# A priority flag on one weight split, and later planner due times for four inverses, in a two-layer decoder trunk

## The chip, the cores and the metric

One core of a Trainium2 chip runs the whole trunk. The metric is the device time of one execution in microseconds (us), as the median of several. TensorE (PE in the rows) multiplies matrices, VectorE (DVE), ScalarE (ACT) and GpSimd (POOL) work element by element, and SyncE (SP) issues the DMAs.

## What is computed

An even layer (RWKV-7 with 16 heads, S5, memory attention) is followed by an odd layer (Mamba-2, latent attention, memory attention). Both have one input projection, one output projection and a residual add; a norm ends the trunk. Model width and sequence length are 1024, all in fp32. The part of the reference that this case turns on is RWKV's step:

```
def step(state, inp):
    r_t, w_t, k_t, v_t, kk_t, b_t = inp
    sa = -jnp.einsum('bhij,bhj->bhi', state, kk_t)
    state = (state * w_t[:, :, None, :] + sa[..., None] * b_t[:, :, None, :]
             + v_t[..., None] * k_t[:, :, None, :])
    return state, jnp.einsum('bhij,bhj->bhi', state, r_t)
```

The kernel does it in blocks of 128 steps. Within a block the dependence on `sa` is a triangular system, and the inverses of its 32x32 diagonal parts are needed before the block's state can be computed.

## The kernel before

**Dense products.** Projections run as fp32 in three products of rounded halves: x is kept as `xhi` and `xlo`, and each 128x512 weight tile `w` is loaded by a DMA (`load_w`, L322), cast to `wh` on ACT (L405) and reduced to the remainder `wl` on DVE (L406; both in `split`). Each step of 128 rows is three matmuls of 128x512 (`mm<-xhi,wh`, `mm<-xlo,wh`, `mm<-xhi,wl`, L180), called *products* below. `w` has two buffers, `wh` and `wl` four each. Eight steps, 24 products, fill one bank "mm" (there are two), which ACT and DVE then evacuate into a tile `ev` (two buffers) that a DMA stores.

**What sets the order.** `Flow` (from L160) plans PE's order by hand: generators ("streams") with ranks yield the event they wait for, `F.done(event, dt)` sets when an event is due, and the clock `now` advances by a cost for each matmul. The stream of the best rank that is due goes next; the dense products, `self.bg` with rank 9 (`dense`, L340), fill what is left. `keep_in_program_order` makes that PE's order on the chip. The other engines and SP's DMA issues are put in order by the framework's scheduler, which goes by dependencies, its own estimates and priorities. On the chip every engine works its list strictly in order and waits wherever an operand is missing.

**The first weight tiles.** `rw_items` (L876) begins the dense list. Its first item takes the tiles 24 and 8, already loaded as `self.w0`, and the tile `win[0]`, the *third*, whose split goes through `load_w`; its products write a bank "g" for the first half of the sequence.

**RWKV's units.** `rw_streams` (L920) works 16 units (head pair p, half h), n = 0 to 15. For each, `stream_a` forms `ga` (`rw_prep0`) and calls `rw_inv0` (L690): SP sends `ga` out to `d_in` (L699, four DMAs) and back in another layout as `ai` (L702), POOL solves by 62 operations on `ti` (L711, L713), SP stores `ti` to `d_out` (L715) and fetches the inverse as `xt` (L718, four DMAs). Then `stream_i` runs `rw_inv1` (L720): DVE transposes `xn<-xt` (L728), and PE's first products with it are `g<-xn,ga`. `stream_b` forms the other operands (transposes of `rv`, `tg`, `km`; copies `tok` on ACT, L684), and `stream_s` runs the recurrence. `stream_a` may start unit n when unit n-3's recurrence is done, because there are three tiles `xt`. The event ("V", n), at which the planner takes unit n's inverse as ready, is due HW = 14 planner microseconds after `pool_t`, which advances by at least HV = 16 for each unit.

**After RWKV.** S5 reads parameters (`s5_params`, products `bbr`, `bbi`, L1307), and `mem_load` (L1033) fetches `mh` and `ml`, 1 MB each, into a pool on the space that S5's temporary tiles leave, so those DMAs wait for the last use of these, DVE's `bbi` of L1307. 24 *memory products* `mm<-mh,wh` (and `ml,wh`, `mh,wl`, 128x256) stand in the dense list, due S5M = 13 planner microseconds after the load was asked for. S5's own first work on PE is transposes `g<-ident,rn` (L184).

Of the kernel before, what the change touches and what calls it, by code (L numbers as in the profile page):

```python
# [19 lines left out]
P = 128  # L20
# [112 lines left out]
HW = 14  # L133
# [26 lines left out]
class Flow:  # L160
# [4 lines left out]
    def __init__(self, tc, banks):  # L165
        self.tc, self.nc = tc, tc.nc
        self.now = 0.0
        self.at, self.streams, self.n = {}, [], 0
        self.banks = banks
        self.free = {t: [0.0] * n for t, n in banks.items()}  # L170
# [76 lines left out]
class Item:  # L247
# [1 line left out]


    def __init__(self, src=None, kt=8, x=None, evac=None, ev=None, m=P, halves=(0, 1), wait=None, hwait={},
                 pre=None, post=None, gen=None, first=True, last=True, kwait={}):
        self.src, self.kt, self.x, self.evac, self.ev, self.m = src, kt, x, evac, ev, m
        self.halves, self.wait, self.hwait, self.pre, self.post, self.gen = halves, wait, hwait, pre, post, gen
        self.first, self.last, self.kwait = first, last, kwait


class Tiles(list):
# [7 lines left out]
class K:  # L266
# [52 lines left out]
        return pool.tile(list(shape), F32, name=tag, bufs=self.flow.banks[tag])  # L319


    def load_w(self, parts, src, kt, m=P, pool=None):  # L322

        nc = self.nc
        src = src.rearrange("p (k m) -> p k m", k=kt)
        ks = 4 * P // m
        for k in range(0, kt, ks):
            n = min(ks, kt - k)
            v = lambda t: t[:, 0:n * m].rearrange("p (k m) -> p k m", k=n)
            w = v(self.wp.tile([P, 4 * P], F32, name="w", bufs=2))  # L330
            nc.sync.dma_start(w, src[:, k:k + n])
            hi, lo = (v((pool or self.wp).tile([P, 4 * P], F32R, name=x, bufs=4 if pool else WB)) for x in ("wh", "wl"))
            self.split(hi, lo, w)
            for p, t in zip(parts, (hi, lo)):
                p.extend(t[:, i] for i in range(n))
            yield k + n

    def dense(self, items):

        F = self.flow  # L340
        acc, w, ends = {}, {}, {}
        live = [0]

        def pieces():
            for n, i in enumerate(items):
                w[n], ends[n] = (Tiles(), Tiles()), []
                if i.src is not None:
                    for e in self.load_w(w[n], i.src, i.kt, i.m):
                        ends[n].append(e)
                        live[0] += 1  # L350
                        yield n if e == i.kt else n - 0.5
                else:
                    yield n
        todo = pieces()
        at = [-1]

        def fill(n):

            while at[0] < min(n, len(items) - 1) or live[0] < WB and at[0] < min(n + 2, len(items) - 1):
                at[0] = next(todo)  # L360

        for n, cur in enumerate(items):
            fill(n)
            if cur.wait is not None:
                yield cur.wait
            if cur.pre:
                cur.pre()
            if cur.gen:
                yield from cur.gen(w[n])
                live[0] -= len(ends[n])  # L370
            else:
                for h in cur.halves:
                    if h in cur.hwait:
                        yield cur.hwait[h]
                    if cur.first:
                        yield ("mm", 1)
                        acc[h] = self.bank("mm")
                    (hi, lo), m, kt = w[n], cur.m, cur.kt
                    for k in range(kt):
                        if k in cur.kwait:  # L380
                            yield cur.kwait[k]
                        if k == 0 or k in cur.kwait:
                            xh, xl = cur.x(h)
                            ps = acc[h][:, 0:xh.shape[-1]]
                        for j, (l, r) in enumerate(((hi, xh), (hi, xl), (lo, xh))):
                            F.matmul(ps[0:m], lhsT=l[:, k], rhs=r[:, k], start=(cur.first and k == 0 and j == 0),
                                     stop=(cur.last and k == kt - 1 and j == 2))
                        if h == cur.halves[-1] and k + 1 in ends[n]:
                            live[0] -= 1
                            fill(n)  # L390
                        if k < kt - 1:
                            yield 0
                    if cur.last:
                        cur.evac(h, ps)
                        F.rel("mm", 2.0)
            if cur.ev:
                F.done(cur.ev, 7.0)
            if cur.post:
                cur.post()
            del w[n]  # L400
            yield 0
# [478 lines left out]
    def rw_items(self, np_, x, rd, zd, npairs=8):  # L880

        nc, F = self.nc, self.flow
        win = self.I["w_ev_in"]
        item = lambda ct, ev: Item(win[ct], 8, x, self.shift_evac(ct, rd[ct]), ev)
        gate = lambda p: Item(win[35 + p], 8, x, self.keep_evac("gate", zd[p]), ("gate", p))

        def first(w):
            evs = [(self.shift_evac(ct, rd[ct], np_.tile([P, 1], F32, name="bd%d" % ct)), ev)
                   for ct, ev in ((24, "lat"), (8, ("k", 0)), (0, None))]
            for h, tags in enumerate((("mm", "mm", "g"), ("g", "mm", "mm"))):  # L890
                yield ("raw", h)
                xh, xl = x(h)
                self.raw[h] = []
                for tag, (hi, lo), e in zip(tags, (*self.w0, w), evs):
                    yield (tag, 1)
                    ps = self.bank(tag)
                    for k in range(8):
                        for j, (l, r) in enumerate(((hi, xh), (hi, xl), (lo, xh))):
                            F.matmul(ps, lhsT=l[:, k], rhs=r[:, k], start=(k == 0 and j == 0), stop=(k == 7 and j == 2))
                        yield 0  # L900
                    self.raw[h].append((ps, tag, *e))
                F.done(("raw1", h))
        items = [Item(win[0], 8, gen=first)]
        for p in range(npairs):
            if p:
                items += [item(8 + p, ("k", p)), item(p, None)]
            items.append(item(16 + p, ("v", p)))
            if p:
                items.append(gate(p - 1))
        items[1].hwait = {0: ("x0", 0), 1: ("x0", 1)}  # L910
        items.append(gate(npairs - 1))
        return items

    def rw_streams(self, cp, wk, rd, zd, npairs=8):


        nc, F = self.nc, self.flow
# [5 lines left out]
        pool_t = [0.0]  # L923
# [9 lines left out]
        def raw(n, nm, c, bufs):  # L933
            p, h = units[n]
            t = self.pp.tile([P, HT], F32, name=nm, bufs=bufs)
            nc.sync.dma_start(t, rd[c + p][:, h * HT:(h + 1) * HT])
            return t

        def latents():

            lat = self.pp.tile([P, T], F32, name="ai", bufs=1)
            nc.sync.dma_start(lat, rd[24])
            nc.scalar.activation(lat[0:64], lat[0:64], AF.Tanh)
            for h in (1, 0):
                s = slice(h * HT, (h + 1) * HT)
                lt = self.pp.tile([P, 2, HT], F32R, name="lt", bufs=1)
                for i, (hs, ls) in enumerate(((slice(0, 64), slice(64, 128)), (slice(64, 128), slice(0, 64)))):
                    nc.scalar.copy(lt[hs, i], lat[hs, s])
                    nc.vector.tensor_tensor(lt[ls, i], lat[hs, s], lt[hs, i].bitcast(F32), A.subtract)
                nc.sync.dma_start(ltd[h], lt.bitcast(F32))  # L950
            return lt

        def stream_a():
            yield "lat"
            lt = latents()
            for n, (p, h) in enumerate(units):
                yield [("k", p), E("S", n - 3), E("B", n - 1)]
                if n % 2 == 0 and n:
                    lt = self.pp.tile([P, 2, HT], F32R, name="lt", bufs=1)
                    nc.sync.dma_start(lt.bitcast(F32), ltd[h])  # L960
                k = raw(n, "rk", 8, 2)
                yield from self.rw_prep0(st[n], p, lt, lora(p), k, wk)
                F.done(("A", n), 2.5)
                self.rw_inv0(st[n], n, wk)
                pool_t[0] = max(pool_t[0], F.now + 10) + HV
                F.done(("V", n), pool_t[0] + HW - F.now)

        def stream_i():
            for n in range(nh):
# [1522 lines left out]
```

## Time and profile before

| | before |
|---|---|
| median of three runs | 2689.26 us (2682.48 to 2698.61) |
| the profiled execution | 2699.3 us, span 2697.5 us |
| granted PE clock, mean | 0.953 of full |
| PE busy | 2520.6 us, 93% |
| DVE, ACT, POOL busy | 66%, 46%, 21% |

PE is busy in 93% of the span, so a change tells in two ways: through the time in which PE stands, and through the time in which it runs at the lower of its two levels (a granted clock of 0.50 is 1.2 GHz, 1.00 is 2.4 GHz). A row of the timeline gives start, duration, engine, line, operation, what it writes and reads, how many were joined (x4), and in brackets how long the engine had stood before it and what released it.

### The profile page before, as it was taken

How to read it: one execution, taken by the hardware profiler on the slowest of the kernel's cores; microseconds unless marked ns; L12 is line 12 of the kernel's file. 1: busy time of each engine (PE TensorE's matmuls, PEld its weight loads, DVE VectorE, ACT ScalarE, POOL GpSimd, SP SyncE). 2: the span in 40 equal slices, each digit the busy share in tenths (PEclk: the TensorE clock that was granted, in tenths of full speed). 3: DMA queues.
4: the chain of work that ended last, by engine and by line, in shares of the span. 5: the costliest groups of instructions: out<-in, count | busy, mean ns of one | idle time of the engine just before them, and what ended most of it. 6: DMA issues, size and time to landing. Idle time of an engine off the chain costs nothing. (4 is left out here: it accounts for less than half of the span.)

```text
span 2697.5 us, 42287 instructions
## 1 busy us (share of the span) xinstructions
PE 2520.6 (93%) x15058; PEld 2036.5 (75%) x15058; DVE 1771.6 (66%) x3639; ACT 1249.7 (46%) x2445; POOL 563.2 (21%) x1287
## 2 busy tenths in 40 slices
PE   7979999999999988988999998999999989999997
PEld 5757777787777867775678776777777768887786
DVE  9846667676666646777556456798644987777432
ACT  7533344343444333455444345545434645666443
POOL 3432353334434410000000111122111120000011
PEclk9988899998999999988999999999999989999999
DMA  4432323333333244464574564252445332114543
GB/s 150 130 93 86 87 83 91 106 103 87 92 97 88 74 128 145 124 205 149 172 255 141 164 187 138 69 128 87 125 146 197 117 109 65 58 51 144 164 135 100
DMA packets 263859, 328.27 MB, mean 122 GB/s; under 512 B 88016, under 2 KB 135248, under 8 KB 263136
## 3 DMA queue, kind: packets, MB, share of 16 engines
q1 hardware_dynamic: 260736, 319.39, 38.5%
q0 software_dynamic: 1280, 4.20, 0.4%
q8 instruction: 119, 1.95, 0.3%
q10 hardware_dynamic: 1632, 1.98, 0.3%
q14 instruction: 92, 0.75, 0.1%
HBM read 232.59 MB, written 92.90 MB: 121 GB/s over the span
## 5 line engine op out<-in xcount | busy, mean ns | idle before, releaser
L406 DVE TENSOR_TENSOR wl<-w,wh 128x512 fp32r<-128x512 f32 (+2 forms) x410 | 273.9, 672 | 295.7 <-ACT wh L405 291.4
L405 ACT CAST wh<-w 128x512 fp32r<-128x512 f32 (+2 forms) x410 | 241.8, 594 | 417.8 <-PE mm L180 259.8
L180 PE MATMUL mm<-xhi,wh 128*128 128x512 f32 x832 | 364.1, 438 | 10.5 <-ACT xhi L474 6.5
L180 PE MATMUL mm<-xlo,wh 128*128 128x512 f32 x832 | 339.7, 408 | 3.8 <-DVE xlo L497 2.4
L180 PE MATMUL mm<-xhi,wl 128*128 128x512 f32 x832 | 338.8, 407 | 0.0
L180 PE MATMUL mm<-x1h,wh 128*128 128x512 f32 (+1 forms) x608 | 249.7, 411 | 23.3 <-ACT craw L1829 16.6
L711 POOL TENSOR_TENSOR titmp<-ai,ti 128x60 f32<-128x60 f32 (+24 forms) x496 | 167.4, 338 | 412.1 <-DMA ai<-d_in 374.5
L180 PE MATMUL mm<-x1h,wl 128*128 128x512 f32 (+1 forms) x608 | 240.9, 396 | 0.0
L180 PE MATMUL mm<-x1l,wh 128*128 128x512 f32 (+1 forms) x608 | 240.7, 396 | 0.0
L180 PEld LDWEIGHTS mm<-xhi,wh 128*128 128x128 f32 x832 | 162.3, 195 | 64.2 <-issue 19.9
L180 PEld LDWEIGHTS mm<-xhi,wl 128*128 128x128 f32 x832 | 162.6, 195 | 39.5
L180 PEld LDWEIGHTS mm<-xlo,wh 128*128 128x128 f32 x832 | 163.2, 196 | 36.0 <-DVE xlo L475 4.9
L713 POOL TENSOR_TENSOR ti<-ti,titmp 128x60 f32<-128x60 f32 (+24 forms) x496 | 171.5, 346 | 38.8
L180 PEld LDWEIGHTS mm<-x1h,wh 128*128 128x128 f32 (+1 forms) x608 | 115.6, 190 | 55.3 <-ACT craw L1829 19.5
L180 PEld LDWEIGHTS mm<-x1l,wh 128*128 128x128 f32 (+1 forms) x608 | 115.7, 190 | 26.6 <-issue 3.2
L180 PEld LDWEIGHTS mm<-x1h,wl 128*128 128x128 f32 (+1 forms) x608 | 115.8, 191 | 26.2 <-DVE wl L406 0.2
L180 PE MATMUL mm<-yb,wh 128*128 128x512 f32 x320 | 102.3, 400 | 4.2 <-ACT yb L405 3.5
L786 DVE TENSOR_TENSOR gb<-g,m 128x256 f32<-128x256 f32 x128 | 49.3, 416 | 62.9 <-PE g L180 62.5
L800 ACT ACTIVATE sn<-s0c,fin 64x64 f32<-64x64 f32 x128 | 44.1, 345 | 98.7 <-DVE s0c L828 55.8
L419 DVE SCALAR_TENSOR_TENSOR ev<-ev,mm 128x512 f32<-128x512 f32 x72 | 49.0, 680 | 45.7 <-ACT ev L418 45.4
L180 PEld LDWEIGHTS mm<-yb,wh 128*128 128x128 f32 x320 | 60.8, 190 | 20.2 <-ACT yb L405 4.0
L180 PE MATMUL g<-xn,ga 32*32 32x32 f32 (+1 forms) x768 | 39.0, 225 | 37.4 <-DVE xn L728 35.4
(597 smaller groups left out, 6241.9 us busy)
## 6 DMA issues: line engine op xcount, KB each, us to landing
w<-in_w_ev_in SPq DMA_DIRECT2D x106, 256.0 KB
w<-in_w_od_in SPq DMA_DIRECT2D x82, 256.0 KB
w<-in_w_ev_out SPq DMA_DIRECT2D x64, 256.0 KB
w<-in_w_od_out SPq DMA_DIRECT2D x64, 256.0 KB
rd<-ev SPq DMA_DIRECT2D x50, 256.0 KB
spl<-yd SPq DMA_DIRECT2D x40, 256.0 KB
zod<-ev SPq DMA_DIRECT2D x36, 256.0 KB
ai<-d_in SPq DMA_DIRECT2D x16, 512.0 KB
```

The costliest lines, as they stand in the source:

```text
L180: return self._pe(self.nc.tensor.matmul(out, lhsT=lhsT, rhs=rhs, start=start, stop=stop, **kw), math.prod(rhs.shape[1:]), rhs.dtype)
L405: self.nc.scalar.copy(hi, src)
L406: self.nc.vector.tensor_tensor(lo, src, hi.bitcast(F32), A.subtract)
L419: nc.vector.scalar_tensor_tensor(g, g, 1.0, ps, A.add, A.mult)
L711: eng.tensor_tensor(tm, ai[:, s:s + 1, s + 1:32].broadcast_to([P, n, w]), ti[:, 0:n, s:s + 1].broadcast_to([P, n, w]), A.mult)
L713: eng.tensor_tensor(ti[:, 0:n, s + 1:32], ti[:, 0:n, s + 1:32], tm, A.subtract)
L786: nc.vector.tensor_tensor(gb[:, h], pgs[h], self.m2, A.mult)
L800: nc.scalar.mul(sg[hs], sc[hs, hs], g[hs])
```

## The change

Two edits. An `Item` has a new flag `soon`; `load_w` wraps the split of such an item in the scheduler's high priority, and the first item of `rw_items`, with the third weight tile, carries it. And ("V", n) is due max(8 - 2n, 0) planner microseconds later: 8, 6, 4 and 2 for units 0 to 3, nothing from unit 4 on. The changed file is one line longer from L331 on.

```
-    def load_w(self, parts, src, kt, m=P, pool=None):
+    def load_w(self, parts, src, kt, m=P, pool=None, soon=False):
...
-            self.split(hi, lo, w)
+            with self.tc.high_priority() if soon else ExitStack():
+                self.split(hi, lo, w)
...
-                    for e in self.load_w(w[n], i.src, i.kt, i.m):
+                    for e in self.load_w(w[n], i.src, i.kt, i.m, soon=i.soon):
...
-        items = [Item(win[0], 8, gen=first)]
+        items = [Item(win[0], 8, gen=first, soon=True)]
...
-                F.done(("V", n), pool_t[0] + HW - F.now)
+                F.done(("V", n), pool_t[0] + HW - F.now + max(8 - 2 * n, 0))
```

**Place 1, the third weight tile, DVE.** The subtractions `wl<-w,wh x2` are those of the third tile's two parts; `xlo` is the low half of x, `l2l` that of a small matrix. Before:

```order
22 L482 TENSOR_TENSOR acc_167<-acc_167,sq_187 128x512
23 L475 SCALAR_TENSOR_TENSOR xlo<-x_190,cols,xhi 128x512 x8
24 L406 TENSOR_TENSOR l2l<-l_649,l2h 128x256
25 L406 TENSOR_TENSOR wl<-w,wh 128x512 x2
26 L488 TENSOR_TENSOR q_345<-mm,r_150 128x512
```

And now:

```order
22 L483 TENSOR_TENSOR acc_167<-acc_167,sq_187 128x512
23 L476 SCALAR_TENSOR_TENSOR xlo<-x_190,cols,xhi 128x512 x8
24 L407 TENSOR_TENSOR l2l<-l_649,l2h 128x256
25 L407 TENSOR_TENSOR wl<-w,wh 128x512 x2
26 L489 TENSOR_TENSOR q_345<-mm,r_150 128x512
```

Nothing moved here; ACT's two casts of the tile stand in the same rows of its list too.

**Place 2, unit 0's inverse, PE and ACT.** PE before, up to the first products with unit 0's inverse (`g<-xn,ga`) and a little behind; `rv` and `tg` are operands of unit 0's recurrence:

```order
446 L180 MATMUL mm<-xhi,wh 128x512
447 L180 MATMUL mm<-xlo,wh 128x512
448 L180 MATMUL mm<-xhi,wl 128x512
449 L180 MATMUL g<-xn,ga 32x32 x16
450 L184 MATMUL g<-ident,rv 128x128 x4
451 L184 MATMUL g<-ident,tg 128x128 x4
```

Now, where `ce`, `cc`, `km` and `kr` belong to unit 0's other operands as well, and the first product of row 457 opens the next "mm" bank (nine more products follow, and `g<-xn,ga 32x32 x16` is row 476):

```order
455 L184 MATMUL g<-ident,rv 128x128 x4
456 L184 MATMUL g<-ident,tg 128x128 x4
457 L180 MATMUL mm<-xhi,wh 128x512
458 L180 MATMUL mm<-xlo,wh 128x512
459 L180 MATMUL mm<-xhi,wl 128x512
460 L180 MATMUL mm<-xhi,wh 128x512
461 L180 MATMUL mm<-xlo,wh 128x512
462 L180 MATMUL mm<-xhi,wl 128x512
463 L180 MATMUL g<-ce,blk 128x512
464 L180 MATMUL g<-cc,blk 128x512
465 L184 MATMUL g<-ident,km 128x128 x4
466 L180 MATMUL g<-kr,tg 128x128 x8
```

ACT around the same work before (`ev<-mm` is the evacuation of a bank, `wh<-w` the cast of a weight tile, `tok` copies the transposes, `zi` the first products with the inverse):

```order
L561 ACTIVATE ev_1429<-mm_1314,omu_86 128x512
L405 CAST wh_1456<-w_1454 128x512
L684 COPY tok_1494<-g_1495 128x512
L739 ACTIVATE zi_1483<-g_1466 32x8x32
L684 COPY tok_1494<-g_1501 128x512
```

And now:

```order
L562 ACTIVATE ev_1429<-mm_1314,omu_86 128x512
L406 CAST wh_1453<-w_1451 128x512
L406 CAST wh_1471<-w_1469 128x512
L562 ACTIVATE ev_1475<-mm_1434,omu_86 128x512
L685 COPY tok_1488<-g_1489 128x512
L685 COPY tok_1488<-g_1495 128x512
```

21 dense products and unit 0's transposes and products with `blk` and `tg` moved ahead of the first use of its inverse. At later units the number of dense products that moved ahead of the first use of the inverse is 27 (unit 1), 12 (2), 63 (3), 57 (4), 45 (5), 63 (6), 60 (7); ahead of the making of `ga` it is 36 for unit 3, 54 for unit 6, 63 for unit 8, and matmuls of other units moved with them. From unit 8's inverse on, every step of RWKV stands exactly 60 dense products further back than before, and from PE row 6060 on (single matmuls counted) both lists are the same again.

**Place 3, the start of S5, PE.** Behind RWKV's last transposes of `ty` come 87 products before, and then the first transposes of S5:

```order
3701 L180 MATMUL mm<-xhi,wh 128x512
3702 L180 MATMUL mm<-xlo,wh 128x512
3703 L180 MATMUL mm<-xhi,wl 128x512
3704 L184 MATMUL g<-ident,rn 128x128 x8
3705 L180 MATMUL mm<-xhi,wh 128x512
```

Now 39 products follow the last `ty`, and then the memory products:

```order
3713 L180 MATMUL mm<-xhi,wh 128x512
3714 L180 MATMUL mm<-xlo,wh 128x512
3715 L180 MATMUL mm<-xhi,wl 128x512
3716 L180 MATMUL mm<-mh,wh 128x256
3717 L180 MATMUL mm<-ml,wh 128x256
```

The 24 memory products stood 12 products behind `rn`; now they stand ahead of it, with 12 products between (`g<-ident,rn` is row 3752).

## Rows read from the trace of the kernel before

**Rows 1.** The page: busy time of each engine, share of the span.

```profile
PE 2520.6 (93%) x15058; PEld 2036.5 (75%) x15058; DVE 1771.6 (66%) x3639; ACT 1249.7 (46%) x2445; POOL 563.2 (21%) x1287
```

**Rows 2.** Waits of PE: total us, times, longest us.

```profile
PE g L180 <- DVE xn L728: 35.4, 21, 7.2
PE g L180 <- DVE wl L406: 5.6, 1, 5.6
```

**Rows 3.** Timeline of DVE and PE at the third weight tile.

```profile
18.57 9.62 DVE L475 SCALAR_TENSOR_TENSOR xlo<-x,cols,xhi 128x512 fp32r<-128x512 f32 x8
29.52 2.35 DVE L406 TENSOR_TENSOR wl<-w,wh 128x512 fp32r<-128x512 f32 x2
31.32 0.80 PE L180 MATMUL g<-xhi,wl 128*128 128x512 f32 x1 [5.57 <-DVE wl L406]
```

**Rows 4.** Timeline of PE at unit 0's inverse.

```profile
136.06 0.40 PE L180 MATMUL mm<-xhi,wl 128*128 128x512 f32 x1
142.94 0.28 PE L180 MATMUL g<-xn,ga 32*32 32x32 f32 x2 [6.48 <-DVE xn L728]
```

**Rows 5.** Timeline of ACT there.

```profile
140.86 0.69 ACT L561 ACTIVATE ev<-mm,omu 128x512 f32<-128x512 f32 x1 [8.85 <-DMA zr<-ev]
144.79 0.62 ACT L405 CAST wh<-w 128x512 fp32r<-128x512 f32 x1 [3.24 <-DMA w<-in_w_ev_in]
```

**Rows 6.** Timeline of SP's DMA issues there.

```profile
135.43 0.57 SPq L715 DMA_DIRECT2D d_out<-ti  x1
...
140.16 1.80 SPq L718 DMA_DIRECT2D xt<-d_out  x4
...
144.50 1.53 SPq L699 DMA_DIRECT2D d_in<-ga  x3
```

**Rows 7.** Timeline of PE at the inverses of units 1, 2, 3, 7 and 8.

```profile
192.98 0.31 PE L180 MATMUL g<-xn,ga 32*32 32x32 f32 x2 [7.25 <-DVE xn L728]
...
248.97 0.22 PE L180 MATMUL g<-xn,ga 32*32 32x32 f32 x2 [1.19 <-ACT ta L616]
...
316.26 0.28 PE L180 MATMUL g<-xn,ga 32*32 32x32 f32 x2 [3.89 <-DVE xn L728]
...
530.77 0.31 PE L180 MATMUL g<-xn,ga 32*32 32x32 f32 x2 [3.44 <-DVE xn L728]
...
581.68 0.69 PE L180 MATMUL g<-xn,ga 32*32 32x32 f32 x32
```

**Rows 8.** SP: the fetch of xt(1), the sends of ga(3) and ga(8).

```profile
190.77 1.81 SPq L718 DMA_DIRECT2D xt<-d_out  x4
...
265.92 2.04 SPq L699 DMA_DIRECT2D d_in<-ga  x4
...
532.88 2.08 SPq L699 DMA_DIRECT2D d_in<-ga  x4
```

**Rows 9.** Windows: us, busy us (and instructions) of PE, PEld, DVE, ACT, POOL, PEclk, DMA share, GB/s.

```profile
46.00:60.00 14.00, 14.00 (x61) 11.28 (x60) 13.91 (x19) 9.73 (x18) 6.31 (x4) 1.00 0.28 100
...
189.00:209.00 20.00, 15.36 (x136) 11.90 (x136) 7.79 (x17) 4.59 (x10) 0.40 (x1) 0.50 0.53 137
```

**Rows 10.** Timeline of PE at the start of S5.

```profile
1037.60 0.60 PE L184 MATMUL g<-ident,ty 128*128 128x128 f32 x4
...
1065.89 1.94 PE L184 MATMUL g<-ident,rn 128*128 128x128 f32 x8 [5.48 <-issue]
...
1071.35 0.28 PE L180 MATMUL mm<-mh,wh 128*128 128x256 f32 x1
...
1074.07 0.28 PE L180 MATMUL mm<-mh,wl 128*128 128x256 f32 x1
```

**Rows 11.** The memory load there: SP's issue, then two windows.

```profile
1054.46 0.32 SPq L1036 DMA_DIRECT2D mh<-mhd  x1
...
1056.00:1064.00 8.00, 3.06 (x12) 2.18 (x12) 8.00 (x14) 5.28 (x10) 0.00 (x0) 0.93 0.92 350
...
1064.00:1066.00 2.00, 0.11 (x1) 0.14 (x2) 2.00 (x5) 0.00 (x0) 0.00 (x0) 0.50 0.37 115
```

More of the change, by code (lines that the diff above doesn't have):

```diff
@@ L251, in __init__ @@
     def __init__(self, src=None, kt=8, x=None, evac=None, ev=None, m=P, halves=(0, 1), wait=None, hwait={},
-                 pre=None, post=None, gen=None, first=True, last=True, kwait={}):
+                 pre=None, post=None, gen=None, first=True, last=True, kwait={}, soon=False):
         self.src, self.kt, self.x, self.evac, self.ev, self.m = src, kt, x, evac, ev, m
         self.halves, self.wait, self.hwait, self.pre, self.post, self.gen = halves, wait, hwait, pre, post, gen
-        self.first, self.last, self.kwait = first, last, kwait
+        self.first, self.last, self.kwait, self.soon = first, last, kwait, soon
 class Tiles(list):
```

## The prediction

> **What bounds the kernel now.** I read the page's busy line first, then PE's list of waits, then the timelines at the places where the two orders differ. PE is busy 2520.6 us of 2697.5 [rows 1]; no work is added or removed, so the change can only move time through PE's standing and PE's lower clock level. PE's costliest wait on another engine is that for the inverses: 35.4 us in 21 pieces [rows 2]. The pieces sit at the first products with an inverse, at units 0, 1, 3 and 7 above all [rows 4, 7]; unit 8 has none [rows 7]. Behind them PE runs at the lower level for a while: 189 to 209 us has a granted clock of 0.50, against 1.00 in an undisturbed stretch [rows 9].
>
> What makes PE wait there is a loop, not one slow step. SP sends `ga` of unit 1 at 144.50, POOL solves, SP fetches the inverse at 190.77 [rows 6, 8], and PE uses it at 192.98 [rows 7]: 48.5 us from send to use, of which PE's order moves nothing. Unit 3's send at 265.92 [rows 8] leads to PE's use at 316.26 [rows 7], 50.3 us. So a unit's inverse is there some 50 us after its `ga` is sent, and the sends wait for `ga`, which PE makes.
>
> **Edit 1, the priority: 0.** The third tile makes PE stand once, 5.57 us at 31.32 [rows 3]. DVE is at x's low halves from 18.57 for 9.62 us, then at `l2l`, and subtracts the third tile only from 29.52 [rows 3]. The wait would go if the subtractions were put ahead of part of those `xlo`. In the new order they stand behind the same eight `xlo` and `l2l`, and ACT's casts stand where they stood. The same list on the same engine gives the same wait. Had it moved, the gain would be bounded by 5.57 us and the slower spacing behind it; none is taken, and the loss is bounded by zero too, since nothing is pushed back.
>
> **Edit 2, unit 0: 0.** PE's wait of 6.48 us at 142.94 [rows 4] goes, as 21 products and unit 0's other matmuls now stand ahead. But 6 products after the last common one PE opens another bank "mm" (there are two), and the bank is freed by the evacuation that ACT begins at 140.86. That waits 8.85 us for the store `zr<-ev` [rows 5], which SP has behind unit 0's `d_out` at 135.43 [rows 6]. The six products take 1.4 us (61 instructions in 14.00 us [rows 9], 0.23 each) and the transposes of `rv` and `tg` about as much, so PE stands from some 139.5 to 141.6. Then `g<-kr,tg` needs ACT's `tok` copies. They now stand behind two casts and one more evacuation, and the first cast gets its weights at 144.79 [rows 5]; the copies end near 148. Two and four us stand in the place of the 6.48: zero, with bounds of -6.5 (nothing replaces the wait) and +3 (all copies late by another weight tile).
>
> **Edit 2, units 1 to 8: +3.** Unit 1's send and fetch stay where they are, while PE has 27 products more to do before it, 6.3 us: of 7.25 us [rows 7] about 1 is left, and PE is 6.3 ahead. The products that moved ahead are not free for the loop, however: `ga` of unit 3 now has 36 products and other units' matmuls before it that stood behind, 14.6 us at the trace's durations. Its send goes from 265.92 [rows 8] by 14.6 - 6.3 to about 274, and unit 3's inverse from 316.26 [rows 7] to about 325, 9 later, with 16.7 us more work done by then (63 products and units' work): still 7.7 ahead. From here each inverse follows from the one before by the loop. Unit 4's comes 9 later with 12.3 of work ahead (PE stands about 5), unit 5's 8.5 later with 9.0. `ga` of unit 6 has 15.2 us more before it, so it is sent 8.5 + 15.2 - 9.0 = 14.7 later; unit 6's inverse finds PE just arriving, and unit 7's, from 530.77 [rows 7] to about 545.5, finds PE standing for some 8 us, since only 11.4 us of work came ahead. Before, that wait was 3.44 [rows 7]. `ga` of unit 8 has 15.7 more before it; its send moves from 532.88 [rows 8] to about 549, unit 8's first use from 581.68 [rows 7] by 17. From there on both orders are the same but for 60 products, 14.0 us [rows 9]. So 17 - 14 = +3 at RWKV's end. Bounds: -6 if the 6.3 of unit 1 is kept to the end (the later sends not late for PE), +10 if the waits at units 4, 5 and 7 each bring a stretch at the lower level such as 189 to 209, where 15.36 us of busy time at 0.50 [rows 9] cost 7.7; one such stretch less at unit 1 is in the lower bound.
>
> **Start of S5: +11.** This is the larger term. Before, from the last `ty` at 1037.60 to `rn` at 1065.89 [rows 10] are 28.3 us; 87 products (20.3 us at 0.233) lie in them, so 8.0 are lost, 5.48 of them right ahead of `rn`. The memory load is issued at 1054.46, as soon as DVE has done with the space it goes to; the stores and loads run at 350 GB/s until 1064 and at 115 behind [rows 11]. So `mh` and `ml` are there at about 1064.2, 26.6 us behind `ty`, and before nobody waits, for the memory products come only at 1071.35 [rows 10]. Now PE has 39 products (9.1 us) behind `ty`, and then the memory products, which it can't pass. It stands from 9 to 26.6. Then come 24 memory products (1071.35 to 1074.07 and 0.28 [rows 10], 3.0 us) and 12 products (2.8), and `rn` at 32.4 at the best, some 34 with the lower level that follows such a stand (0.50 from 1064 to 1066 [rows 11], behind 5.48 of standing). Its work is 14.9, lost are 17.5 to 19, against 8.0: +9.5 to +11, and I take +11. Bounds: +6 where the load starts earlier, since fewer evacuations stand in DVE's list ahead of `bbi`, +15 where the lower level lasts through all 14.9 us of work. The cover that the load had, 87 products, is what the shift by 60 has used up.
>
> The Trainium skill, in "DMA: Bandwidth & Descriptors" (section "Anatomy of one DMA — SWDGE (gpsimd) path"), fits the time of a transfer as 2.0 us and its bytes by 436 GB/s. By that, an estimate, the two loads together (2 MB) would take 6.8 us and land 3 us earlier, and the sum would be 3 us smaller; the trace's 350 GB/s, shared with weights and stores [rows 11], speaks for the longer time.
>
> **Behind it: 0.** The rest of S5 has the same matmuls, in another order up to PE row 6060 and the same order from there. 24 fewer products are left to fill S5's gaps; I take 0, with bounds of 6 on both sides, the size of one wait such as 5.48 [rows 10].
>
> **Sum.** 0 + 0 + 3 + 11 + 0 = +14 on the profiled execution's 2699.3 us. The median is 2689.3, 10 lower, and the difference goes on the median: 2703.
>
> **Rivals.** (A) *The waits go and the lower level with them.* Units 0, 1, 3 and 7 stand 6.5, 7.3, 3.9 and 3.4 us [rows 4, 7], 21 together; if each also has a stretch such as 189 to 209 behind it, whose 15.36 busy us at 0.50 cost 7.7 [rows 9], the full level there brings back up to 31 more: -52, with the 11 of S5 -41, 2648 (without S5's loss 2637). It decides at unit 3: it holds if `ga` of unit 3 is sent no later than before. For it: the inverse is late, and PE gets work to do in the time. Against it: the work put ahead stands ahead of later `ga` as well, and POOL's loop has no slack. It is the rival that ends faster.
>
> The Trainium skill, "TensorE: Matmul & The Clock Gate" (section "Terms"), puts the penalty of the lower level at the time spent there times one half, which is how (A) counts it; the stretch 189 to 209 is at 0.50 [rows 9].
>
> (B) *The memory load is not waited for.* If DVE's `bbi` and with it the load come some 15 us earlier behind `ty`, only the +3 is left: 2692, no change. For it: DVE has fewer splits and evacuations ahead of `bbi`. Against it: S5's parameters come only when RWKV's space is free, and 16.9 us pass between `ty` and the issue.
>
> (C) *More is lost in the loop.* Each of units 4, 5 and 7 gets a stand of 5 to 8 us and a lower level behind it: +10 in place of +3, and S5's at its upper end: +25, 2714.
>
> (D) *The change does nothing*: excluded for edit 1's order, not for edit 2, whose order differs in thousands of rows.
>
> **Numbers.** What a measurement of this kernel can tell from no change is about 0.5%, 13.4 us: 2675.8 to 2702.7. The forecast (2695 to 2709 with its smaller spreads) gets 0.50, (B) 0.22, (C) 0.16, (A) 0.12. Of the forecast's half, about half lies above 2702.7; with (C) this gives 0.41 slower; (B) and the other half give 0.47 the same; (A) 0.12 faster. The range leaves out (A), and (C)'s upper part: 2683 (both RWKV bounds and (B): -6) to 2719.
>
> **What would show it.** In the changed profile: PE's wait for `wl` near 31 unchanged at 5.6 (edit 1); the wait at unit 0's inverse gone, but waits on ACT for a bank and `tok` between 138 and 149; unit 1's inverse used at about 193 with a wait under 2; unit 3's at about 325, unit 7's with a wait near 8, unit 8's near 599. At S5's start a wait of PE for a DMA of some 17 us at the first memory product. If that is missing, the main term is wrong; if unit 3's `ga` is sent before 268, the loop's is.

## The result: slower by 1.2%

| | before | changed |
|---|---|---|
| median of the compared runs | 2693.94 us | 2722.82 us (2720.26 to 2735.2) |
| ratio, 95% interval | | 1.0118 [1.0089, 1.0147] |
| the profiled execution | 2699.3 us | 2724.63 us, span 2722.9 |
| PE busy | 2520.6 us | 2516.4 us |

The forecast was 2703 (2683 to 2719), +14 us. Measured are +28.9 us between the medians (that of the kernel before now takes in a fourth run, 2698.88) and +25.3 between the two profiled executions. The direction was right, and the time lies outside the range. PE's busy time fell by 4 us while the span grew by 25, so on balance the loss is standing, and not a lower clock.

Waits of PE in the changed kernel (total us, times, longest us), to be read against [rows 2]:

```profile
PE g L180 <- DVE xn L729: 31.1, 18, 5.5
...
PE mm L180 <- ACT sn L1215: 10.6, 1, 10.6
...
PE g L180 <- DVE s0c L829: 7.2, 1, 7.2
...
PE g L180 <- DVE wl L407: 5.6, 1, 5.6
```

The wait for the third tile's `wl` is the same 5.6 us. The waits for the inverses fell only from 35.4 to 31.1 us, and new names stand beside them. PE's timeline at units 0, 1, 2, 3, 7 and 8, answering [rows 4, 7]:

```profile
142.87 0.77 PE L180 MATMUL mm<-xhi,wh 128*128 128x512 f32 x1 [3.47 <-DVE ev L567]
...
148.06 1.64 PE L180 MATMUL g<-kr,tg 64*128 64x128 f32 x16 [1.22 <-ACT tok L685]
...
198.97 0.80 PE L180 MATMUL g<-s0c,kr 128*128 128x128 f32 x2 [7.16 <-DVE s0c L829]
199.69 0.31 PE L180 MATMUL g<-xn,ga 32*32 32x32 f32 x2
...
245.11 0.31 PE L180 MATMUL g<-xn,ga 32*32 32x32 f32 x2 [3.11 <-DVE xn L729]
...
322.53 0.63 PE L184 MATMUL g<-ident,ty 128*128 128x128 f32 x4 [4.07 <-DVE ty L852]
...
330.31 0.24 PE L180 MATMUL g<-xn,ga 32*32 32x32 f32 x2 [0.70 <-DVE xn L729]
...
549.65 0.28 PE L180 MATMUL g<-xn,ga 32*32 32x32 f32 x2 [4.18 <-DVE xn L729]
...
555.66 0.79 PE L180 MATMUL g<-kr,tg 64*128 64x128 f32 x2 [4.02 <-DVE rk L626]
...
610.32 0.78 PE L180 MATMUL g<-xn,ga 32*32 32x32 f32 x32
```

SP's sends of unit 3's and unit 8's `ga` in the changed kernel, answering [rows 8]:

```profile
275.33 1.80 SPq L700 DMA_DIRECT2D d_in<-ga  x4
...
559.63 1.80 SPq L700 DMA_DIRECT2D d_in<-ga  x4
```

Where the time went is read by comparing the moments at which both kernels reach the same point, and crediting each dense product done earlier with 0.2333 us:

| point | before | changed | products ahead | net |
|---|---|---|---|---|
| unit 1's inverse used | 192.98 | 199.69 | +27 | +0.4 |
| unit 2's | 248.97 | 245.11 | +12 | -6.7 |
| unit 3's | 316.26 | 330.31 | +63 | -0.6 |
| unit 7's | 530.77 | 549.65 | +60 | +4.9 |
| unit 8's | 581.68 | 610.32 | +60 | +14.6 |
| last `ty` | 1037.60 | 1065.85 | +60 | +14.2 |
| first `rn` | 1065.89 | 1097.15 | +24, and 24 memory products | +22.8 |
| end of the span | 2697.5 | 2722.9 | 0 | +25.4 |

So RWKV cost 14.2 us in this pair of executions, the start of S5 8.6, and the rest 2.6. The net counts dense products alone. Matmuls of the units moved too: priced at the durations of the kernel before, an estimate, they would make the net -4.3 at unit 2, -2.2 at unit 3 and +6.3 at unit 7; at units 1 and 8 and at the last `ty` they are the same in both.

Windows of the changed kernel from the use of unit 4's inverse to unit 5's and from unit 7's to unit 8's (us, busy us of PE, PEld, DVE, ACT, POOL, then PE's granted clock, DMA share, GB/s):

```profile
376.10:431.80 55.70, 53.13 (x382) 41.75 (x383) 31.72 (x74) 18.98 (x43) 20.36 (x63) 0.86 0.35 100
549.70:610.30 60.60, 55.61 (x419) 45.35 (x419) 41.78 (x97) 23.37 (x50) 21.49 (x63) 0.87 0.31 95
```

And the same stretches of the kernel before:

```profile
369.00:421.50 52.50, 49.45 (x404) 39.65 (x405) 35.52 (x82) 21.12 (x46) 20.59 (x63) 1.00 0.30 89
530.80:581.70 50.90, 50.20 (x387) 40.43 (x387) 36.77 (x85) 20.34 (x45) 20.56 (x63) 0.94 0.34 100
```

The stands at later units bring lower-level stretches that were not there before: 0.86 against 1.00, 0.87 against 0.94. The stretch from unit 1's inverse to unit 2's is the other way round (0.95 from 199.7 to 245.1 us, 0.85 from 193 to 249 before), so the clock as a whole is no worse: 0.954 in the changed kernel, 0.953 before.

At S5's start, answering [rows 10, 11], PE first, then DVE's last step for `rn`, then SP's issue of the memory load:

```profile
1065.85 0.60 PE L184 MATMUL g<-ident,ty 128*128 128x128 f32 x4
...
1086.15 0.55 PE L180 MATMUL mm<-mh,wh 128*128 128x256 f32 x1 [10.60 <-ACT sn L1215]
...
1088.80 0.58 PE L180 MATMUL mm<-ml,wh 128*128 128x256 f32 x1 [2.10 <-DMA ml<-mhd]
...
1097.15 1.04 PE L184 MATMUL g<-ident,rn 128*128 128x128 f32 x8
```

```profile
1090.32 1.29 DVE L1362 TENSOR_TENSOR rn<-rn,rn 128x512 f32<-128x512 f32 x2
```

```profile
1080.88 0.32 SPq L1037 DMA_DIRECT2D mh<-mhd  x1
1081.24 0.42 SPq L1037 DMA_DIRECT2D ml<-mhd  x1
```

PE stands 12.7 us there in place of 5.48. The name "ACT sn" in the first row is the event seen last; the twin stand in a run below is put down to the load of `mh`.

### The profile page after: what moved, and what is told of

Same layout as the page of the kernel before. It is cut to its first block, busy times and chain, and to the rows that moved or that the text cites. A ratio compares the mean times of both kernels' runs of the same rounds, so it can differ in the third digit from the quotient of the medians.

```text
span 2722.9 us, 42261 instructions
## 1 busy us (share of the span) xinstructions
PE 2516.4 (92%) x15058; PEld 2029.7 (75%) x15058; DVE 1771.3 (65%) x3639; ACT 1244.4 (46%) x2440; POOL 562.7 (21%) x1287
## 5 line engine op out<-in xcount | busy, mean ns | idle before, releaser
L180 PEld LDWEIGHTS mm<-x1h,wl 128*128 128x128 f32 (+1 forms) x608 | 116.1, 191 | 27.6 <-DVE wl L407 1.4
L2235 ACT ACTIVATE pe<-g,lmx 128x512 f32<-128x512 f32 (+2 forms) x96 | 55.4, 583 | 35.4 <-DVE lmx L2232 34.4
```

The costliest lines, as they stand in the source:

```text
L180: return self._pe(self.nc.tensor.matmul(out, lhsT=lhsT, rhs=rhs, start=start, stop=stop, **kw), math.prod(rhs.shape[1:]), rhs.dtype)
L2235: nc.scalar.activation(pe[:, a:b], sc[:, 0:b - a], AF.Exp, bias=mx[:, 0:1], scale=scale, accum_out=sm[:, j:j + 1])
```

## The experiments

### Each edit, and each half of the second, alone

The first edit alone is the change without the new term in the due time.

```
-                F.done(("V", n), pool_t[0] + HW - F.now + max(8 - 2 * n, 0))
+                F.done(("V", n), pool_t[0] + HW - F.now)
```

> The first edit alone: the flag and the scheduler's high priority on the third weight tile's split, the due times as before. The forecast's reason (the split stands in the same rows of DVE's and ACT's lists): nothing moves, ratio to before 1.000 (within 0.003), and PE's wait for wl near 31 us is again 5.6 us. Rival: the priority also gives other instructions another place and carries part of the change's +29 us; then the ratio is above 1.004.

Measured: 0.9996 [0.9974, 1.0018], and PE's row of the wait for the third tile reads as in the changed kernel, 5.6 us. In its trace the five engines run the same instructions as in the kernel before, in the same order but for a few small ones whose records overlap. The priority moves nothing.

Unit 0's delay alone, in the kernel before:

```
-                F.done(("V", n), pool_t[0] + HW - F.now)
+                F.done(("V", n), pool_t[0] + HW - F.now + (8 if n == 0 else 0))
```

> Of the second edit only unit 0's later due time (+8), no flag. The order has 45 products more ahead of RWKV's end and, as in the changed kernel, the memory products ahead of S5's first transposes. If the start of S5 costs what the two traces say (net +12 us between the last ty and rn), that term is here in full, and the total is +12 plus a loop term between -6 and +11 us: ratio 1.002 to 1.009. Rival, everything by the loop in RWKV and nothing by S5's start: the ratio follows the shift, 45/60 of the change's +25 to +29 us, +20, 1.008, and PE has no wait over 3 us for the memory load.

Measured: 1.006 [1.0031, 1.0088], +16 us by the ratio. RWKV costs nothing here: at the last `ty` (1047.38) it is 9.8 us later with 45 products, 10.5 us, more done. S5's start costs 5.9, half of what was expected. PE's stand there:

```profile
1068.93 0.55 PE L180 MATMUL mm<-mh,wh 128*128 128x256 f32 x1 [8.35 <-DMA mh<-mhd]
1071.86 0.58 PE L180 MATMUL mm<-ml,wh 128*128 128x256 f32 x1 [2.37 <-DMA ml<-mhd]
```

The rest, 7 us in the profiled execution, lies behind it and is not explained.

Units 1 to 3 alone:

```
+                F.done(("V", n), pool_t[0] + HW - F.now + (max(8 - 2 * n, 0) if n else 0))
```

> Of the second edit only the later due times of units 1 to 3 (+6, +4, +2), no flag. 24 products more ahead of RWKV's end, and the memory products stay behind S5's first transposes. If S5's start is lost through the memory products' place, the S5 term is absent: 0 to +2 us there, and the total is the loop term alone, -6 to +6 us, ratio 0.998 to 1.002. Rival, the loss is the loop's and goes with the shift: 24/60 of +25 to +29 us, +10, ratio 1.004.

Measured: 1.0012 [0.9987, 1.0038]. The ratio is as expected, but the reason given was wrong: the order puts the memory products ahead of `rn` here too. With 75 products left behind the last `ty` they are no loss (7.6 us lost in the gap, 8.0 before). So the place of the memory products alone does not cost the 8.6 us; how many products are left does. This was the first sign that the forecast's cause at S5's start was wrong. (The profiled execution, 2718.88, is the longest of the ten and 14.8 us above their median; its extra time lies behind `rn`.)

The two halves alone do not add up to the change within RWKV. Net of products, the last `ty` is at -0.7 us with unit 0's delay and at +2.8 with that of units 1 to 3 (1045.97, 24 products ahead), against +14.2 with both. The place where they differ is unit 8's send: it comes 1.6 us behind the first use of unit 7's inverse with unit 0's delay, 1.4 ahead of it with the other half, and 2.1 behind it before, but 10.0 behind it in the changed kernel and in the two kernels below that have its order there.

### What PE waits for at S5's start

The changed kernel with the memory products due later:

```
-S5M = 13
+S5M = 26
```

> The changed kernel with one constant more: the memory products are due 26 planner microseconds after their load is asked for, in place of 13. Up to RWKV's end the order is that of the changed kernel; behind it the memory products stand behind S5's first transposes, as before. If PE's stand for the memory load is the S5 term, it goes: about 12 us less than the changed kernel, +13 to +17 us against before, ratio 1.005 to 1.0065. Rival: S5's first transposes are late for a reason of their own (their parameters, DVE), and PE stands there just as long: ratio as the changed kernel's, 1.010 or more.

Measured: 1.0191 [1.0134, 1.0247], +51 us by the ratio: slower still, and the rival holds. PE no longer meets the memory products, and stands longer, for `rn`, which DVE has ready only then (PE's row, then DVE's):

```profile
1096.92 1.30 PE L184 MATMUL g<-ident,rn 128*128 128x128 f32 x5 [15.79 <-issue]
```

```profile
1096.03 1.28 DVE L1362 TENSOR_TENSOR rn<-rn,rn 128x512 f32<-128x512 f32 x2
```

From the last `ty` to `rn` are 25.5 us here. DVE's chain (the store of `ty` frees space, the parameters are loaded into it, DVE computes from them) takes about that long here whether or not PE has the memory products ahead of `rn`. To test it, DVE was made to work out the first `rn` ahead of `car`, `cat` and `cai`, some 5 us of work that stood ahead of it, with PE's order the same; once in the kernel before, once on top of the last one.

```
-        tt = nc.vector.tensor_tensor
+        tt0 = nc.vector.tensor_tensor
+        tt = (lambda *z: F.tc.keep_in_program_order(tt0(*z))) if ct == 0 else tt0
```

> The kernel before with one thing forced: at S5's start DVE makes the tiles rn of the first column ahead of car, cat and cai (some 5 us of DVE's work that stood ahead of rn); PE's order is the same. If PE stands at S5's start for DVE's rn and for nothing else, its wait of 5.48 us falls to about 0.5 and the time by 4 to 6 us: ratio 0.998. Rival: car and cai are then late for the next products and the time comes back: ratio 1.000.

> The changed kernel with the memory products due later (26) and DVE's rn put ahead of car, cat and cai as well. The run with the memory products later showed PE standing 15.8 us for rn. If it is DVE's chain from the last ty to rn, no longer covered by dense products, that stand falls by about 5 us, to 10 or 11, and the ratio from 1.019 to about 1.017. If the stand were for a DMA (the parameters, S5's input), it stays at 15 to 16.

Measured: 0.9993 [0.9973, 1.0014] and 1.0152 [1.0113, 1.0191]. The stands moved about as expected. PE's wait for `rn` in the kernel before with `rn` first:

```profile
PE g L184 <- DVE rn L1344: 1.5, 1, 1.5
```

And in the other, where 15.8 was:

```profile
PE g L184 <- ACT cs L1217: 10.6, 1, 10.6
...
PE g L184 <- DVE rn L1345: 1.3, 1, 1.3
```

(In the 10.6 the event seen last is ACT's `cs`, which ended at 1081.75; DVE had the first part of `rn` ready at 1081.59.) So the stand is DVE's chain: with the chain 5 us shorter, the stands are 4 us shorter and the gap from the last `ty` to `rn` 5 to 6 us. The whole time of the kernel before did not fall by as much as the measurement can tell: the interval of 0.9993 holds the 4 to 6 us hoped for (0.9978 to 0.9985), and it holds the rival, no gain. In the profile `rn` comes 5.9 us sooner behind the last `ty`, and the span is 1.1 us longer all the same, so that the gain comes through to the end is not shown.

The gap in all these profiles, last `ty` to first `rn` (work: 0.2333 us for each product, 0.1185 for each memory product; of the 24 memory products three have no record in the row with 21; with `rn` first the gap ends at the first of its two parts, and the second is 2 us behind):

| kernel | gap | products + memory products | work | lost |
|---|---|---|---|---|
| before | 28.3 | 87 + 0 | 20.3 | 8.0 |
| before, `rn` first | 22.4 | 87 + 0 | 20.3 | 2.1 |
| units 1 to 3 alone | 27.6 | 75 + 21 | 20.0 | 7.6 |
| unit 0 alone | 32.1 | 66 + 24 | 18.2 | 13.9 |
| changed | 31.3 | 51 + 24 | 14.7 | 16.6 |
| changed, memory later | 25.5 | 39 + 0 | 9.1 | 16.4 |
| the same, `rn` first | 20.3 | 39 + 0 | 9.1 | 11.2 |

The gap has a floor of 25 to 28 us set by DVE; the loss is what the products left do not fill. In the changed kernel the memory products add to it: `rn` was ready at 1091.6 and PE took it at 1097.15.

Why the kernel with the memory products later lost 22 us more than the changed kernel is only in part clear: at `rn` its profile stands at +28.2 net against +22.8, and that difference was there at RWKV's end already, with the same order up to there, so it is one execution against another; the rest, some 16 us, came behind `rn`, where S5's work is in another order. The longest single stands of PE there are 8.2 us for the DMA `toe<-kd` and 5.7 for DVE's `ks`; no run tests them.

### Is the loss in RWKV the loop's?

GpSimd's solve was cut to 16 of its 31 steps in both kernels, which leaves out the rest of the inverse; PE's and DVE's orders stay.

```
-        for s in range(31):
+        for s in range(16):
```

> The kernel before with GpSimd's solve cut short: 16 of its 31 steps, 32 of 62 operations for each unit (the rest of the inverse is left out); PE's and DVE's orders stay. Each inverse is there some 12 us earlier. If the loop of send, solve and fetch sets RWKV's pace, PE's 35 us of waits for the inverses fall below 10 and the lower level behind them goes too: 35 to 60 us less, ratio 0.978 to 0.987. Rival, the waits only move to the next operand: under 15 us less, ratio above 0.994.

> The changed kernel with the same cut (16 of 31 steps of the solve, the rest of the inverse left out). If the +11 us that the change costs within RWKV are the loop's, they go when the loop is short: the difference to the cut kernel before is what is lost behind RWKV, +12 to +16 us, ratio to before 0.983 to 0.992. Rival, RWKV's +11 are stands for banks and copies (ACT, SP) that the loop has no part in: the difference to the cut kernel before stays at +25 to +29 us.

Measured: 0.9771 [0.9736, 0.9806] and 0.9826 [0.9797, 0.9856], each just beyond the fast end of what was expected. The medians are 2635.37 and 2654.68, and by the ratios (times 2698) the two cut kernels are 15 us apart. (The +11 and +12 of the expectations are a first count of the terms that stand as 14.2 and 8.6 above.) Since the first profile of the cut kernel before lay 19 us above its own median, both were profiled once more.

> The kernel before with 16 of the 31 steps of each solve (the rest left out), looked at once more, since the profiled execution of the first look lay 19 us above the median. If the change's RWKV term is the loop's, the cut kernels' difference at the last ty, net of 60 products, is again zero or below (-8 in the first look). The first execution was a slow sample if the last ty now comes 10 us or more before 986.

> The changed kernel with the same cut, looked at once more. With the loop as the cause the last ty comes no later than the other's plus 14 us (60 products); with stands that the loop has no part in, it comes 25 us or more later.

The second profiles, PE's waits for the inverses in the cut kernel before, and then in the changed one:

```profile
PE g L180 <- DVE xn L728: 2.9, 4, 1.2
```

```profile
PE g L180 <- DVE xn L729: 2.7, 3, 1.9
```

At the last `ty` the cut kernels are at 979.41 and 991.14: +11.7 us with 60 products, 14.0 us, more done, net -2.3 (-8.4 in the first profiles). The cut kernel before came there 7.1 us earlier than in its first profile, where 10 were set as the sign that the first one had been long. From the last `ty` to `rn` 8.2 and 16.1 us are lost, as in the uncut kernels.

How far one profile can be trusted is seen from kernels with the same order up to the last `ty`. It comes at 1037.60, 1043.41 (first edit alone) and 1039.08 (`rn` first) with the order of the kernel before, and at 1065.85, 1071.43 and 1061.53 with that of the changed kernel (the two others have the memory products later). Net of 60 products the means are 12.2 us apart, and the nearest two 4.1. The cut kernels are at -2.3 and -8.4. So the loss within RWKV is there only while the loop is long: it is the loop's, and it is some 12 us, give or take 5. The S5 term stays, so it is not. What stays open is the time of the cut kernels: the second profiles, 2638.95 and 2645.37, are 6 us apart where the medians are 19 apart.

### Shortening the loop in earnest

Leaving out half the solve gave 62 us, so two ways were tried to have some of that with the full result. First, the last 15 steps of the solve on VectorE, then the whole of it.

```
+            if s == 16:
+                eng = nc.vector
```

```
-        eng = nc.gpsimd
+        eng = nc.vector
```

> The kernel before with the last 15 of the 31 steps of each solve moved from GpSimd to VectorE (same arithmetic, PE's order unchanged). Leaving these steps out gave ratio 0.977. If the loop's length is what PE pays for, and DVE (66% busy, 0.16 to 0.2 us for such small operations against 0.3 on GpSimd) does the 30 operations in 5 to 8 us between its other work, a third to two thirds of those 62 us are had: ratio 0.983 to 0.993. Rival: DVE's own queue delays both the solve and the splits behind it, and the gain is lost: 0.998 to 1.01.

> The kernel before with the whole solve on VectorE. DVE then has 62 dependent operations more for each unit, 10 to 12 us of its time, 160 to 190 us in all, in a stretch where it is busy for two thirds. If the loop's length counts more than DVE's load, ratio 0.975 to 0.99; if DVE's load counts, the splits wl and the evacuations come late for PE and the ratio is 1.00 to 1.03.

Measured: 1.0801 [1.0775, 1.0828] and 1.0771 [1.0738, 1.0803], 8% slower, far beyond the rivals' bounds too. The operation itself is faster on VectorE, as the row of the products `titmp` shows (ns, least/median/most), a median of 214 against 296 on GpSimd in the kernel before:

```profile
L711 DVE TENSOR_TENSOR titmp<-ai,ti x496: 111/214/238, 106.2 to 1159.7; 128x60 f32<-128x60 f32 x16, 128x28 f32<-128x28 f32 x12, 128x66 f32<-128x66 f32 x11, 128x48 f32<-128x48 f32 x10
```

But VectorE works its list in order, and now stands in it: for GpSimd's half in the one kernel, for the fetch of `ai` in the other.

```profile
DVE titmp L713 <- POOL ti L715: 190.2, 15, 28.2
```

```profile
DVE titmp L711 <- DMA ai<-d_in: 123.7, 15, 13.2
```

PE's wait for the inverses rises to 173.4 us in the second. Nor is the solve itself shorter there: it takes 15.2 us at the five units where its operations stand together in VectorE's list, but 32.7 to 44.4 at nine of the sixteen, where 24 to 33 us of VectorE's other work stand between them. On GpSimd it takes 24.1 to 28.7. GpSimd stood 374.5 us for the fetches of `ai` in the kernel before; at most units its list holds nothing but the solve (63 instructions), so that no other work stood behind them. A list of VectorE that keeps every solve together was not tried.

Second, the two outward transfers on other queues: `d_in` sent by ScalarE, and `ai` fetched by GpSimd in one of the two kernels.

```
-            nc.sync.dma_start(d_in[i]...
+            nc.scalar.dma_start(d_in[i]...
-        nc.sync.dma_start(ai.rearrange("p s t -> p (s t)"), ...
+        nc.gpsimd.dma_start(ai.rearrange("p s t -> p (s t)"), ...
```

> The kernel before with the loop's two outward steps on other queues: d_in is sent by ScalarE right behind its copy of ga (4 sends a unit), and ai is fetched by GpSimd, which stands idle for it anyway; PE's order is unchanged. In the kernel before, unit 1's ga was copied by 132 us but sent only at 144.5, since SP had the end of unit 0's solve ahead of it; at units 2, 4, 7 and 8 that gap is 10, 8, 3 and 7 us. If the loop sets RWKV's pace, inverses come up to 10 us earlier, PE's 35 us of waits for them fall below 15, and the ratio is 0.98 to 0.992. Rival: GpSimd's own fetch is slow (it makes the descriptors itself) or the four sends hold up ScalarE's casts, and the ratio is 0.998 or more.

> The kernel before with only d_in on ScalarE's queue; ai stays on SP. If SP's standing for the solve's end is what delays the send, this alone gives most of the gain, ratio 0.985 to 0.995; if SP then stands for the fetch of ai just as long, it gives nothing, 0.998 to 1.002.

Measured: 1.0032 [0.9998, 1.0066] and 0.9994 [0.9964, 1.0023]: nothing gained. In the kernel with both transfers moved ScalarE has `ga` of unit 1 by 132.8 and sends it at 145.10, as late as SP did (ACT, then SP):

```profile
131.73 1.07 ACT L654 COPY ga<-g 128x512 f32<-128x512 f32 x2
145.10 2.22 ACTq L699 DMA_DIRECT2D d_in<-ga  x4
147.42 0.69 ACT L561 ACTIVATE ev<-mm,omu 128x512 f32<-128x512 f32 x1 [14.62 <-DMA d_in<-ga]
```

```profile
143.28 1.80 SPq L718 DMA_DIRECT2D xt<-d_out  x4
```

With `d_in` alone on ScalarE's queue it goes at 141.12, 3.4 us earlier, but PE's waits for the inverses are 39.5 us:

```profile
141.12 2.62 ACTq L699 DMA_DIRECT2D d_in<-ga  x4
```

```profile
138.75 1.80 SPq L718 DMA_DIRECT2D xt<-d_out  x4
```

In both it goes out just behind the fetch `xt` of unit 0, though the queues differ. The trace says why: SP's DMAs and these sends share eight semaphores, and a send first waits for the earlier transfer on its own. With `d_in` alone moved the first send has the semaphore of the second of the four fetches of `xt`; that one's last update is at 141.05, and the wait ends at 141.07. That the time would fall with semaphores of their own was not tested. No version with the whole inverse beat the kernel before by more than can be measured.

## Why the prediction was wrong

**Edit 1, right.** Same rows in the list, same wait of 5.6 us, ratio 0.9996.

**Unit 0, right in kind.** The wait of 6.48 became stands for the bank (3.47) and for `tok` (1.22), and unit 0's inverse was used 9 us later than before with 21 products, 4.9 us, and unit 0's own matmuls done ahead.

**Unit 1, wrong.** The step that leaves about 1 of the 7.25 us and puts PE 6.3 ahead failed. The wait for the inverse fell to nothing, but PE stood 7.16 for `s0c` instead, the state of a recurrence that the new order sets right ahead of it; DVE made it at 198.34, behind an evacuation. Unit 1's inverse was used at 199.69, not 193, net +0.4 in place of -6.3. At unit 2 most of the 6 us were there (net -6.7, or -4.3 with the units' matmuls counted), one unit late.

**Units 3 to 8, right in kind, mis-sized.** The forecast had unit 3's send at 274, its use at 325, unit 7's use at 545.5 with a stand of 8, unit 8's send at 549 and its use at 599. Measured: 275.3, 330.3, 549.7 with 4.2, 559.6 and 610.3. The loop's length was right: 50.7 us from unit 8's send to the use of its inverse, where some 50 were taken. The step that failed is the send itself, 10.6 us later than forecast; unit 8's use follows it. I priced it by the PE work ahead of unit 8's `ga`, and left out what that `ga` now stands behind. DVE in the changed kernel, then ACT and SP:

```profile
549.08 1.45 DVE L729 STREAM_TRANSPOSE xn<-xt 32x256 f32<-32x256 f32 x3 [10.36 <-DMA xt<-d_out]
...
554.91 0.69 DVE L626 TENSOR_TENSOR rk<-ta,rk 128x512 f32<-128x512 f32 x1
```

```profile
558.53 1.07 ACT L655 COPY ga<-g 128x512 f32<-128x512 f32 x2
```

```profile
547.32 1.80 SPq L719 DMA_DIRECT2D xt<-d_out  x4
```

And PE, ACT and SP in the kernel before, where the products for unit 8's `ga` ran ahead of unit 7's inverse:

```profile
523.73 1.06 PE L180 MATMUL g<-kr,tg 64*128 64x128 f32 x16
```

```profile
524.82 1.07 ACT L654 COPY ga<-g 128x512 f32<-128x512 f32 x2 [1.25 <-PE g L180]
```

```profile
528.58 1.81 SPq L718 DMA_DIRECT2D xt<-d_out  x4
```

DVE stands 10.36 us for unit 7's inverse, and the operands of unit 8's `ga` (up to `rk`) come behind it; PE's `g<-kr,tg` for that `ga` stands behind `g<-xn,ga` of unit 7 too, and waits 4.02 for `rk`. Before, `ga` of unit 8 was copied by 525.9, ahead of that inverse. So the change put the making of `ga` 8 inside the loop, behind inverse 7: the send follows the fetch of unit 7's inverse by 12.3 us where it was 4.3. Of the 10.6 us, 4.2 are unit 7's inverse used later than forecast and 4.0 PE's stand for `rk`. Rival (C), "more is lost in the loop", +10, was the nearer one within RWKV, and by this pair of profiles its +10 was still 4 short.

**S5's start, the size nearly right, the cause wrong.** Forecast +11, measured +8.6. That the cover of 87 products had been used up was right, and PE did stand at the first memory product. The step "`mh` and `ml` are there at about 1064.2, 26.6 us behind `ty`" failed: PE used `mh` 20.3 us behind it, 5.3 us after its issue, and `ml` 23.0 behind it, 7.6 us after its own issue; the load was also issued sooner, 15.0 us behind `ty` in place of 16.9. I had read the load's end from the total DMA rate of a window in which weights and stores moved as well. By the fit of the Trainium skill's "DMA: Bandwidth & Descriptors" (section "Anatomy of one DMA — SWDGE (gpsimd) path"), which is for DMAs that GpSimd issues, the two take an estimated 6.8 us. Here SyncE issues them, and PE used `ml` 7.9 us after the first issue, between that and my 9.7. Nor does the window from 1064 to 1066 at 0.50 lie behind the stand of 5.48, as I read it: it lies within it, for PE stood until 1065.89. And the memory load was not what mattered: with it out of the way PE stood as long for DVE's `rn`, a wait that I had put at nothing. The products that used to cover DVE's chain had been spent in RWKV. That the size came out near is in part luck, since two stands of like length lay over each other.

**Behind it, within its bounds:** 0 forecast, +2.6 measured in this pair of profiles.

The sum failed mainly by RWKV: +3 forecast, +14.2 measured (12.2 between the means of three executions each). Another 4.6 of the 19.8 us between 2703 and 2722.82 are the median of the kernel before, 2693.94 in the compared runs and 2689.3 in the forecast. Rival (A) is excluded: the waits for the inverses fell by 4 us, not by 21.

## What to carry to other kernels

A wait that a loop of transfers and a slow solver sets does not go away when the main engine gets other work ahead of it: what moved ahead also stands ahead of the next round's input, on every in-order engine that makes it, so check each of them for where it would stand. Filler work is a stock: what is spent to cover one wait is missing at the next place that has nothing else to run, and that place has to be found before the stock is spent. A transfer's end is shown by a user that waits for it; where none waits, as in the kernel before, the total rate while others share the queues is only a bound.

## What was not expected of the hardware

GpSimd's standing was useful: moving the same small operations to an engine that does each in 214 ns instead of 296 made the kernel 8% slower, since that engine's list is needed by PE and it now held the waits of 123.7 to 190.2 us, while the rest of the list stretched the solve to as much as 44.4 us. And a send moved to another engine's queue left hardly sooner, or no sooner (141.12 and 145.10, against 144.50 [rows 6]), in both cases just behind the transfer whose semaphore it took over and with which it had nothing else to do.
